# Scatter of experts 24 to 27, the overflow branch and the row loads moved ahead of the up products of experts 28 to 31

## The chip, the cores and the metric

The kernel runs on one core of a Trainium2 chip. A core has a tensor engine (PE; its weight loads are shown as PEld), a vector engine (VectorE, DVE), a scalar engine (ScalarE, ACT), GpSimd (POOL), a sync engine that issues most transfers (SP), and 16 DMA engines. The metric is device microseconds of one execution; lower is better.

## The reference, cut to what matters

Two layers follow each other. Each ends in a mixture of experts: every one of 384 tokens goes to the best two experts of one of four groups (32 experts in all, 1024 wide, 128 hidden), and the result is added to the residual and normalised.

```python
    hid = jax.nn.silu(jnp.einsum('td,edf->tef', t, w1)) * jnp.einsum('td,edf->tef', t, w3)
    hid = hid * gate[..., None].astype(hid.dtype)
    return jnp.einsum('tef,efd->td', hid, w2).reshape(B, L, D)
...
    y = hier_moe(x * (1 + sc2) + sh2, *moe_params)
    x = layer_norm(ALPHA * x + g2 * y, ln2_g, ln2_b)
```

## The kernel before, in words

`experts(l)` handles the experts in eight groups of four, q = 0 to 7. Each expert has room for 32 tokens; up to two experts of a group have a second 32. For each group:

- `ups(q, ...)` makes the up products in four steps (`up`, lines 1409 and 1415). VectorE and ScalarE first copy the weights of the two fuller experts into a buffer `hv` (line 1400).
- `hidden` is SiLU on ScalarE and a product on VectorE (line 1425); `hidden_T` transposes it on PE (lines 1430 and 1432) and VectorE copies it back as `hidT` (line 1436).
- `down(q)` makes three down products: z = 0 and z = 1 (line 1446) and the second slots, called z = 2 here (line 1453). ScalarE takes z = 0 from PSUM, VectorE z = 1, and ScalarE the second slots into the one buffer `ys2` (`y2` in the code). GpSimd scatters the rows by indirect DMA to `y_d` in memory (line 1458). As `ys2` has one buffer, the `y2` of a group is not written before the scatter of the `y2` before it has landed.

The tensor engine's order in the expert stage is the order of the code; for the other engines a scheduler sets it at build time from its own estimate of times. So a copy or a `y2` can stand far from its place in the code.

In the loop `ups(q)` stands ahead of `down(q - 1)`. The last group (q = 7) is different: its rows are not scattered. `down_keep(7)` keeps them in SBUF (`ysk`), and PE adds them by one-hot products (lines 1581 and 1583) to the three 128-token blocks. All other rows come back from memory: `load_yy` loads `y_d` into three tiles `yy` (line 1676), two rows a token. `ln2` adds the pairs (line 1691; one half on GpSimd, one on VectorE), adds PE's sums (line 1732) and normalises.

Between the last scatter and `load_yy` stands `overflow`: a branch (lines 1606 and 1607), taken only when an expert has more tokens than its slots hold. With these inputs it is not taken. Every engine loads the value and branches by itself. In the arm that is not taken each engine waits until its own earlier work is done, and then raises its semaphores by as much as the skipped body would have done.

Weights come in halves of 1 MB, the up weights into pools `raw` (6 buffers) and `wx` (4), the down weights `w2` into `wr` and one more buffer.

Of the kernel before, what the change touches and what calls it, by code (L numbers as in the profile page):

```python
# [8 lines left out]
F32 = mybir.dt.float32  # L9
# [11 lines left out]
D = 1024  # L21
NP, NS, T = 128, 256, 384
NT = 3
# [3 lines left out]
NQUAD = 8  # L27
# [52 lines left out]
class Kern:  # L80
# [1266 lines left out]
    def experts(self, l):  # L1347
        nc, mo, ep, tc = self.nc, self.mo, self.ep, self.tc
# [18 lines left out]
        def windows(q, ns=range(6)):  # L1367

            w = win[q]
            for n in ns:  # L1370
                at = first[4 * q + n] if n < 4 else more[q, n - 4]
                o, i_ = w[:, :, n * 32:(n + 1) * 32], xT[:, :, bass.ds(at, 32)]
                if n < 4:
                    self.act(o, i_, AF.Copy)
                else:
                    nc.vector.tensor_copy(o, i_)
            return w
# [50 lines left out]
        def hidden_T(hid):  # L1428
            pt = self.bank("ms")
            nc.tensor.transpose(pt[:, 0:128], hid[:, 0:2, :].rearrange("p h f -> p (h f)"), self.ident)  # L1430
            for h in range(2):
                nc.tensor.matmul(pt[h * 64:(h + 1) * 64, 128:192].rearrange("p (i r) -> p i r", i=2), hid[:, 2, :], ident4[:, :, h, :],
                                 start=True, stop=True)
            self.hidn += 1
            hT = hidTs[:, self.hidn % 2 * 192:self.hidn % 2 * 192 + 192]
            nc.vector.tensor_copy(hT, pt[:, 0:192])
            return hT
# [72 lines left out]
        def ups(q, kqs):  # L1510
            for kq in kqs:
                up(ps[q], q, kq, win[q])

        ps = {}
        with tc.manual_schedule(engines={e.engine for e in (nc.vector, nc.scalar, nc.tensor)}):
# [17 lines left out]
            hid = hidden(ps[0])  # L1533
            ups(1, (1,))
            hT = hidden_T(hid)
# [10 lines left out]
        with tc.manual_schedule(engines={nc.tensor.engine}):  # L1546
            self.slots()
            hid = hidden(ps[1])
            for z in range(4):
                evac(2, z, "AVAV"[z])  # L1550
            wn = self.hp.tile([128, 2, 8, 192], F32, tag="H", name="win")
            win += [wn[:, q % 2] for q in range(2, NQUAD)]
            windows(2)
            down(0, hT)
            for q in range(2, NQUAD):
                ps[q] = self.bank("mm")
                ups(q, (0, 1))
                hT = hidden_T(hid)
                ups(q, (2, 3))
                hid = hidden(ps[q])  # L1560
                if q < NQUAD - 1:
                    windows(q + 1)
                down(q - 1, hT)
            q, hT = NQUAD - 1, hidden_T(hid)
        self.ahead = self.NRAW
        self.overflow(l)
        self.load_yy(l)

        oT = [ep.tile([128, T], F32R, tag="hv", name="oT", bufs=2), self.eq.tile([128, 2, T], F32R, tag="ys", name="oT", bufs=2)]
        oT = [oT[0], oT[1][:, 0, :], oT[1][:, 1, :]]  # L1570
# [4 lines left out]
        ps = [[self.bank(("tp", "mm", "sc")[i]) for z in range(2)] for i in range(NT)]  # L1575
        with tc.manual_schedule(engines={nc.tensor.engine}):
            for i in range(NT):
                for z in range(2):
                    c = slice(i * 128, (i + 1) * 128)
# [24 lines left out]
    def overflow(self, l):  # L1604
        nc, a, mo, ep, tc = self.nc, self.a, self.mo, self.ep, self.tc
        most = nc.values_load(self.most[0:1, 0:1], min_val=0, max_val=T + CAP + 6 * CAP * T)
        with tc.If(most > 2 * CAP):
            wo = self.wrp.tile([128, 2048], F32, tag="wr", name="wo")
            part = lambda c, n: wo[:, c:c + NT * n].rearrange("p (i e) -> p i e", i=NT)
# [20 lines left out]
            for i in range(NT):  # L1630
                t = tt[:, 1, i, :]
                for d in range(8):
                    ps = self.bank("tp")
                    nc.tensor.transpose(ps[:, 0:128], t[:, d * 128:(d + 1) * 128], self.ident)
                    nc.vector.tensor_copy(tT[i][:, d * 128:(d + 1) * 128], ps[:, 0:128])
            with tc.For_i(0, NQUAD, 1) as it:
                nc.vector.tensor_copy(ixc, ix[:, :, bass.ds(it * 4, 4)])
                nc.vector.tensor_copy(gwc, gw[:, :, bass.ds(it * 4, 4)])
                w = [self.wx.tile([128, 2048], F32, tag="wx", name="w_ov") for _ in range(4)]
                for h in range(4):  # L1640
                    nc.sync.dma_start(w[h], a["w13"][bass.ds(it * 2 + (l * NHALF + h // 2), 1), h % 2].rearrange("o p c -> p (o c)"))
                w2 = [self.rawp.tile([128, 2048], F32, tag="raw", name="w2_ov") for _ in range(2)]
                for z in range(2):
                    nc.sync.dma_start(w2[z], a["w2"][bass.ds(it * 2 + (l * NHALF + z), 1)].rearrange("o p c -> p (o c)"))
                for e in range(4):
                    for i in range(NT):
                        ps = self.bank("mm")
                        for k in range(8):
                            c = e * 512 + k % 2 * 256
                            nc.tensor.matmul(ps[:, 0:256], tT[i][:, k * 128:(k + 1) * 128], w[k // 2][:, c:c + 256],  # L1650
                                             start=k == 0, stop=k == 7)
                        pv = ps[:, 0:256].rearrange("p (h m f) -> p h m f", h=2, m=2)
                        hid = ep.tile([128, 2, 64], F32, tag="hid", name="hidov", bufs=1)
                        self.act(hid, pv[:, :, 0, :], AF.Silu)
                        nc.vector.tensor_tensor(hid, hid, pv[:, :, 1, :], op=ALU.mult)
                        pt = self.bank("ms")
                        nc.tensor.transpose(pt[:, 0:128], hid.rearrange("p h f -> p (h f)"), self.ident)
                        hT = wo[:, 256:384]
                        nc.vector.tensor_copy(hT, pt[:, 0:128])
                        yo = wo[:, 1024:1024 + D]  # L1660
                        yv = yo.rearrange("p (h z c) -> p h z c", h=2, z=2)
                        for z in range(2):
                            po = self.bank("sc")
                            nc.tensor.matmul(po, hT, w2[z][:, e * 512:(e + 1) * 512], start=True, stop=True)
                            nc.vector.tensor_scalar(yv[:, :, z, :], po.rearrange("p (h c) -> p h c", h=2), gwc[:, i, e:e + 1], None, op0=ALU.mult)
                        nc.gpsimd.indirect_dma_start(
                            out=self.y_d, out_offset=bass.IndirectOffsetOnAxis(ap=ixc[:, i, e:e + 1], axis=0),
                            in_=yo, in_offset=None, bounds_check=2 * T - 1, oob_is_err=False)


    def load_yy(self, l):
        nc = self.nc
        self.yy = []
        for i in range(NT):
            t = self.rawp.tile([128, 2, D], F32, tag="raw", name="yy")
            nc.sync.dma_start(t, self.y_d.rearrange("(c t) d -> t c d", c=2)[i * 128:(i + 1) * 128])
            self.yy.append(t)

    def ln2(self, l, ps):
        nc, a, sm = self.nc, self.a, self.sm  # L1680
# [292 lines left out]
```

## Time and profile before

| what | us |
|---|---|
| median of 3 runs (lowest, highest) | 1128.95 (1126.01, 1133.52) |
| the profiled execution's own time | 1127.33 |
| its span, first to last instruction | 1125.6 |
| PE busy, share of the span | 1011.2, 90% |
| DVE busy, share of the span | 810.7, 72% |

The profiled execution is 1.62 us under the median; 1.73 us of its time lie outside the span. Busy times add over the engines, which work side by side; an idle engine costs time only where the end waits for it.

### The profile page before, as it was taken

To read this page: it belongs to the slowest core of one execution; us is meant where nothing else is said; L and a number is where in the kernel's file an instruction comes from. 1 tells how busy PE (TensorE), PEld (TensorE's weight loads), DVE (VectorE), ACT (ScalarE), POOL (GpSimd) and SP (SyncE) were. 2 spreads that over 40 slices of the span, in tenths; PEclk is the share of its full clock that TensorE was granted. 3 is DMA by queue.
4 is the path that set the end of the run, shared out by engine and by line. 5 is a ranking of instruction groups with operands and counts; after the bars stand their busy time and mean duration, and the time that the engine had idled before them with its cause. 6 is when DMAs were issued, how large, how long until landed. Compare 5 with 4: busy or idle time off the path is not lost. (4 is left out here: it accounts for less than half of the span.)

```text
span 1125.6 us, 20806 instructions
## 1 busy us (share of the span) xinstructions
PE 1011.2 (90%) x8182; PEld 840.7 (75%) x8182; DVE 810.7 (72%) x1530; ACT 417.4 (37%) x753; POOL 269.7 (24%) x232
## 2 busy tenths in 40 slices
PE   7999999999999999776689998999999999778673
PEld 5898978877999988433259897788999998754322
DVE  4399999965446986762569999997834587777437
ACT  4324254434333324341163443445532341434221
POOL 0001431221100510333244043114111025013335
PEclk9999999999999989897989999999999999989888
DMA  9967668447436667799585756773223666689955
GB/s 358 412 241 257 266 217 294 178 163 270 151 112 246 259 262 293 303 420 403 219 315 201 280 217 233 251 290 127 110 94 132 224 244 229 227 317 416 419 204 194
DMA packets 55101, 282.75 MB, mean 251 GB/s; under 512 B 8060, under 2 KB 12284, under 8 KB 27857
## 3 DMA queue, kind: packets, MB, share of 16 engines
q1 hardware_dynamic: 49632, 270.01, 63.1%
q0 software_dynamic: 5360, 11.29, 2.7%
q8 instruction: 69, 1.13, 0.4%
q14 instruction: 40, 0.32, 0.1%
HBM read 262.13 MB, written 24.71 MB: 255 GB/s over the span
## 5 line engine op out<-in xcount | busy, mean ns | idle before, releaser
L97 PE MATMUL ps_mm<-hThi,wr 128*128 128x384 f32 x672 | 229.9, 343 | 4.4 <-ACT hThi L102 2.3
L110 DVE TENSOR_TENSOR wr<-w_raw,wr 128x1024 fp32r<-128x1024 f32 x124 | 162.2, 1309 | 92.4 <-ACT wr L102 92.3
L98 PE MATMUL ps_mm<-hTlo,wr 128*128 128x384 f32 x672 | 228.0, 340 | 0.6 <-DVE hTlo L441 0.4
L99 PE MATMUL ps_mm<-hThi,wr 128*128 128x384 f32 x672 | 227.5, 339 | 0.6 <-DVE wr L110 0.6
L102 ACT ACTIVATE wr<-w_raw 128x1024 fp32r<-128x1024 f32 x140 | 147.5, 1055 | 68.1 <-PE ps_mm L99 37.8
L505 DVE SCALAR_TENSOR_TENSOR cacc<-pad,par,cacc 128x399 f32<-128x399 f32 x240 | 169.2, 705 | 4.2
L97 PEld LDWEIGHTS ps_mm<-hThi,wr 128*128 128x128 f32 x672 | 127.1, 189 | 18.2 <-issue 4.0
L98 PEld LDWEIGHTS ps_mm<-hTlo,wr 128*128 128x128 f32 x672 | 127.1, 189 | 6.3 <-DVE hTlo L441 2.5
L99 PEld LDWEIGHTS ps_mm<-hThi,wr 128*128 128x128 f32 x672 | 127.2, 189 | 2.5 <-DVE wr L110 0.9
L110 POOL TENSOR_TENSOR wr<-w_raw,wr 128x1024 fp32r<-128x1024 f32 x10 | 24.5, 2447 | 201.6 <-ACT wr L102 201.2
L1458 POOL DMA_INDIRECT y_d<-ys,dst x28 | 28.4, 1016 | 172.3 <-DVE hv L1400 73.3
L1446 PE MATMUL ps_sc<-w,hidT 128*32 128x512 f32 x256 | 43.1, 766 | 28.6 <-ACT ys L102 21.9
L1415 PE MATMUL ps_mm<-hv,win 128*32 128x128 f32 x1024 | 46.4, 277 | 9.2 <-DVE hv L1400 7.8
L1400 DVE COPY hv<-w_raw 128x512 f32 x60 | 41.9, 737 | 16.6 <-PE ps_mm L1415 10.8
L1415 PEld LDWEIGHTS ps_mm<-hv,win 128*32 128x32 f32 x1024 | 35.8, 112 | 22.7 <-DVE hv L1400 12.0
L1409 PE MATMUL ps_mm<-w_raw,win 128*32 128x256 f32 x640 | 47.8, 391 | 3.5 <-ACT win L102 3.5
L219 PE MATMUL ps_ms<-w_raw,cT 128*32 128x512 f32 x320 | 48.7, 612 | 1.4 <-DMA w_raw<-in_wada 1.4
L102 ACT ACTIVATE gate<-ps_mm 128x384 f32<-128x384 f32 x40 | 19.6, 490 | 81.6 <-PE ps_mm L99 80.5
L1446 PEld LDWEIGHTS ps_sc<-w,hidT 128*32 128x32 f32 x256 | 8.2, 123 | 45.8 <-ACT ys L102 32.9
L911 POOL TENSOR_TENSOR rtmp<-sc,lb 128x1024 f32<-128x1024 f32 x4 | 9.8, 2478 | 121.8 <-DMA lb<-in_ln 121.8
L842 POOL TENSOR_TENSOR merged<-merged,gate 128x384 f32<-128x384 f32 x16 | 18.1, 1135 | 87.0 <-DVE gate L841 87.0
L102 ACT ACTIVATE win<-xT 128x256 f32 x64 | 21.5, 409 | 37.6 <-PE ps_mm L1409 30.2
(505 smaller groups left out, 2355.7 us busy)
## 6 DMA issues: line engine op xcount, KB each, us to landing
w_raw<-in_wst SPq DMA_DIRECT2D x68, 1024.0 KB, 6.4
w_raw<-in_wada SPq DMA_DIRECT2D x48, 1024.0 KB, 5.4
w_raw<-in_w SPq DMA_DIRECT2D x40, 1024.0 KB, 10.7
w<-in_w SPq DMA_DIRECT2D x32, 1024.0 KB, 12.3
w_x<-in_w SPq DMA_DIRECT2D x24, 1024.0 KB, 11.8
bias<-in_bias SPq DMA_DIRECT2D x8, 768.0 KB, 7.6
y_d<-zero SPq DMA_DIRECT2D x2, 3072.0 KB, 15.1
yy<-y_d SPq DMA_DIRECT2D x6, 1024.0 KB, 7.1
```

Of the source, the lines that this page charges most:

```text
L97: mm(out, whi, xhi, start=first, stop=False)
L98: mm(out, whi, xlo, start=False, stop=False)
L99: mm(out, wlo, xhi, start=False, stop=last)
L102: return self.nc.scalar.activation(out, in_, f, **k)
L110: (eng or self.nc.vector).tensor_tensor(lo, x, hi.bitcast(F32), op=ALU.subtract)
L219: nc.tensor.matmul(ps[32 * t:32 * t + 32, :], self.cT[:, 2 * kp + k, :], w[:, t * 512:t * 512 + 512], start=(kp == 0 and k == 0), stop=(kp ...
L505: nc.vector.scalar_tensor_tensor(acc, pad[:, j:j + W], w, acc, op0=ALU.mult, op1=ALU.add)
L1400: nc.vector.tensor_copy(hv[:, i, :], src)
L1409: nc.tensor.matmul(ps[e * 32:(e + 1) * 32, 0:256], x[:, k, e * 32:(e + 1) * 32], w[:, e, kk, :], start=k == 0, stop=k == 7, skip_group_che ...
L1415: nc.tensor.matmul(ps[t * 32:(t + 1) * 32, 256:384], x[:, k, 128 + i * 32:160 + i * 32], hv[:, i, kk, h * 128:(h + 1) * 128], start=False, ...
L1446: nc.tensor.matmul(po[e * 32:(e + 1) * 32, :], hT[:, e * 32:(e + 1) * 32], w2[:, e, :], start=True, stop=True)
L1458: ins = nc.gpsimd.indirect_dma_start(out=view, out_offset=bass.IndirectOffsetOnAxis(ap=dst, axis=0), in_=rows, in_offset=None, bounds_chec ...
```

## The change

The last group's up products no longer stand between group 5's and group 6's down products. After the change PE runs `down(5)`, `hidden_T`, `down(6)`, the branch, `ups(7)`, `hidden_T`, `down_keep(7)`. The loads of `yy` are written ahead of `ups(7)` too. The tiles of `yy` are allocated earlier, and the body of the branch, which isn't run here, uses them for its weights.

```diff
-            for q in range(2, NQUAD):
+            last = NQUAD - 1
+            for q in range(2, last):
                 ps[q] = self.bank("mm")
                 ups(q, (0, 1))
                 hT = hidden_T(hid)
                 ups(q, (2, 3))
                 hid = hidden(ps[q])
-                if q < NQUAD - 1:
-                    windows(q + 1)
+                windows(q + 1)
                 down(q - 1, hT)
-            q, hT = NQUAD - 1, hidden_T(hid)
-        self.ahead = self.NRAW
+            down(last - 1, hidden_T(hid))
+
+        self.yy = [self.rawp.tile([128, 2, D], F32, tag="raw", name="yy") for _ in range(NT)]
         self.overflow(l)
         self.load_yy(l)
+        with tc.manual_schedule(engines={nc.tensor.engine}):
+            ps[last] = self.bank("mm")
+            ups(last, range(4))
+            q, hT = last, hidden_T(hidden(ps[last]))
+        self.ahead = self.NRAW
...
     def overflow(self, l):
...
+        spare = self.rawp.tile([128, 2048], F32, tag="raw", name="w_ov")
+        w = [t.rearrange("p c d -> p (c d)") for t in self.yy] + [spare]
+        w2 = [self.wx.tile([128, 2048], F32, tag="wx", name="w2_ov") for _ in range(2)]
         with tc.If(most > 2 * CAP):
```

On PE, layer 0, from the end of `down(5)` to the branch. Before (`w_5354` and `w_5356` are group 6's down weights, `w_x` and `w_raw` group 7's up weights):

```order
L1415 MATMUL ps_mm<-hv,win 32x128 [waits Activation_49]
...
L1409 MATMUL ps_mm<-w_raw,win 32x256 [waits DMAHW3_49]
...
L1446 MATMUL ps_sc<-w_5354,hidT 32x512 [waits DMAHW4_49,DVE_49]
L1446 MATMUL ps_sc<-w_5354,hidT 32x512 x3
L1446 MATMUL ps_sc<-w_5356,hidT 32x512 [waits DMAHW5_49,Activation_49]
L1453 MATMUL ps_sc<-hv,hidT 32x256 [waits DVE_49]
L1430 MATMUL ps_ms<-con,hid 128x128
L1432 MATMUL ps_ms<-con,hid 64x64 x2
L1606 TENSOR_LOAD most [waits DVE_49]
L1607 COMPARE_AND_BRANCH
```

After, the same place and on to the first up product of group 7 (the branch is lines 1612 and 1616 there):

```order
L1430 MATMUL ps_ms<-con,hid 128x128
L1432 MATMUL ps_ms<-con,hid 64x64 x2
L1446 MATMUL ps_sc<-w_5354,hidT 32x512 [waits DMAHW4_49,DVE_49,Activation_49]
L1446 MATMUL ps_sc<-w_5356,hidT 32x512 [waits DMAHW5_49,Activation_49]
L1453 MATMUL ps_sc<-hv,hidT 32x256 [waits DVE_49]
L1612 TENSOR_LOAD most [waits DVE_49]
L1616 COMPARE_AND_BRANCH
...
L1616 UNCONDITIONAL_BRANCH [waits PE_49]
L1409 MATMUL ps_mm<-w_x,win 32x256 [waits DVE_49,DMAHW6_49,PE_49,Activation_49]
L1409 MATMUL ps_mm<-w_x,win 32x256 x7
L1415 MATMUL ps_mm<-hv,win 32x128 x8
```

All of group 7's up products went behind the branch, and the first of them now waits for ScalarE's semaphore. In the built program this wait asks for a count of 350; ScalarE's last instruction ahead of the branch brings the count to 339, and ScalarE's own not-taken arm then adds 12. The product's PSUM bank is one that the skipped body reads on ScalarE.

On ScalarE, layer 0, up to the branch. Before (`ys_5345`, `ys_5480` and `ys_5605` are the `y2` of groups 4, 5 and 6; the `ys` of size 128x2x256 is z = 0 of group 6; ISA sets a register):

```order
L102 ACTIVATE hv<-w_x 128x512 [waits DVE_49,DMAHW7_49,PE_49,Activation_49]
L102 ACTIVATE ys_5345<-ps_sc,gate 128x512 [waits DMASW0_49,Activation_49]
L102 ISA
L102 ACTIVATE hv<-w_raw 128x512 [waits DMAHW2_49,DVE_49,PE_49]
L102 ACTIVATE hid<-ps_mm 128x192 [waits PE_49]
...
L102 ACTIVATE hv<-w_5356 128x512 [waits DMAHW5_49,DVE_49,Activation_49]
L102 ACTIVATE ys<-ps_sc,gate 128x2x256 [waits DMASW7_49,PE_49]
L102 ACTIVATE ys_5480<-ps_sc,gate 128x512 [waits DMASW2_49,Activation_49]
L102 ACTIVATE ys_5605<-ps_sc,gate 128x512 [waits DMASW4_49,PE_49,Activation_49]
L1606 TENSOR_LOAD most [waits DVE_49]
```

After (`ys_5525` is the `y2` of group 6):

```order
L102 ACTIVATE hv<-w_5356 128x512 [waits DVE_49,DMAHW5_49,PE_49,Activation_49]
L102 ACTIVATE ys_5345<-ps_sc,gate 128x512 [waits DMASW0_49,Activation_49]
L102 ACTIVATE ys<-ps_sc,gate 128x2x256 [waits DMASW7_49,PE_49]
L102 ISA
L102 ACTIVATE hv<-w_x 128x512 [waits DVE_49,DMAHW7_49,PE_49,Activation_49]
L102 ACTIVATE ys_5480<-ps_sc,gate 128x512 [waits DMASW2_49,Activation_49]
L102 ACTIVATE ys_5525<-ps_sc,gate 128x512 [waits DMASW4_49,Activation_49]
L1612 TENSOR_LOAD most [waits DVE_49]
L1616 COMPARE_AND_BRANCH
...
L102 ACTIVATE hv<-w_raw 128x512 [waits DMAHW2_49,DVE_49,PE_49]
L102 ACTIVATE hid<-ps_mm 128x192 [waits DVE_49,PE_49]
```

The second copy and the SiLU of group 7 went behind the branch and so behind the three `y2`, each of which waits (DMASW) for the scatter before it to land. Outside this stage the scheduler also puts instructions of layer 1's mixer in a slightly other order on all engines; which work is done is the same.

## Rows read from the trace of the kernel before

**Rows 1.** Timeline of PE, layer 0: start, duration, engine, line, operation, idle before.

```profile
533.28 1.07 PE L1409 MATMUL ps_mm<-w_raw,win 128*32 128x256 f32 x16
...
535.90 1.04 PE L1446 MATMUL ps_sc<-w,hidT 128*32 128x512 f32 x8
...
539.70 1.07 PE L1453 MATMUL ps_sc<-hv,hidT 128*32 128x256 f32 x16 [0.88 <-DVE ys L1473]
...
544.15 3.60 PE L1446 MATMUL ps_sc<-w,hidT 128*32 128x512 f32 x16 [2.86 <-PEq L1607]
```

**Rows 2.** Timeline of ScalarE, the same stretch.

```profile
529.71 0.63 ACT L102 ACTIVATE hv<-w_x 128x512 f32 x1 [4.91 <-PE ps_sc L1453]
530.25 0.67 ACT L102 ACTIVATE ys<-ps_sc,gate 128x512 f32<-128x512 f32 x1
...
538.52 0.69 ACT L102 ACTIVATE ys<-ps_sc,gate 128x512 f32<-128x512 f32 x1 [0.82 <-DMA y_d<-ys,dst]
545.07 0.69 ACT L102 ACTIVATE ys<-ps_sc,gate 128x512 f32<-128x512 f32 x1 [5.86 <-DMA y_d<-ys,dst]
```

**Rows 3.** Timeline of GpSimd, the same stretch: scatters of groups 4 to 6, a pair sum.

```profile
531.19 0.98 POOL L1458 DMA_INDIRECT y_d<-ys,dst  x1 [1.84 <-ACT ys L102]
...
541.66 1.18 POOL L1458 DMA_INDIRECT y_d<-ys,dst  x1 [0.30 <-issue]
546.03 0.98 POOL L1458 DMA_INDIRECT y_d<-ys,dst  x1 [3.18 <-ACTq L1607]
...
557.54 2.19 POOL L1691 TENSOR_TENSOR yy<-yy 128x512 f32<-128x512 f32 x1 [0.91 <-DMA yy<-y_d]
```

**Rows 4.** SyncE's queue, layer 0: load of `w_5356`, loads of `yy`.

```profile
509.75 0.33 SPq L342 DMA_DIRECT2D w<-in_w  x1
...
549.81 1.42 SPq L1676 DMA_DIRECT2D yy<-y_d  x3
```

**Rows 5.** Transfers issued from 506 to 512 us: count, KB each, median us to landing.

```profile
w<-in_w SPq DMA_DIRECT2D x2, 1024.0 KB, 21.0
```

**Rows 6.** The branch's own instructions, both layers: count, ns min/median/max, first and last start.

```profile
L1607 PEldq COMPARE_BRANCH  x2: 3342/3381/3420, 540.4 to 1085.8; - x2
...
L1607 ACTq EVENT_SEMAPHORE  x2: 17/17/17, 545.9 to 1091.2; - x2
```

**Rows 7.** Timeline of VectorE, layer 0.

```profile
536.52 0.35 DVE L1425 TENSOR_TENSOR hid<-hid,ps_mm 128x192 f32<-128x192 f32 x1
...
542.25 0.34 DVE L1436 COPY hidT<-ps_ms 128x192 f32<-128x192 f32 x1
...
554.79 0.69 DVE L1691 TENSOR_TENSOR yy<-yy 128x512 f32<-128x512 f32 x1 [3.58 <-DMA yy<-y_d]
555.59 0.69 DVE L1732 TENSOR_TENSOR x<-ps_tp,yy 128x512 f32<-128x512 f32 x1
...
558.53 1.75 DVE L1691 TENSOR_TENSOR yy<-yy 128x512 f32<-128x512 f32 x1
560.20 2.28 DVE L1701 SCALAR_TENSOR_TENSOR x<-r,x 128x1024 f32<-128x1024 f32 x1
...
563.93 1.23 DVE L1701 SCALAR_TENSOR_TENSOR x<-r,x 128x1024 f32<-128x1024 f32 x1
```

**Rows 8.** Timeline of all engines, the same place in layer 1.

```profile
1090.45 0.69 ACT L102 ACTIVATE ys<-ps_sc,gate 128x512 f32<-128x512 f32 x1 [6.67 <-DMA y_d<-ys,dst]
...
1090.62 3.55 PE L1446 MATMUL ps_sc<-w,hidT 128*32 128x512 f32 x16 [3.83 <-DVEq L1607]
...
1099.78 0.69 DVE L1691 TENSOR_TENSOR yy<-yy 128x512 f32<-128x512 f32 x1 [1.42 <-DMA yy<-y_d]
...
1100.58 0.69 DVE L1732 TENSOR_TENSOR x<-ps_tp,yy 128x512 f32<-128x512 f32 x1
```

**Rows 9.** Stretches: busy time by engine, granted PE clock (1.00 full), DMA share, GB/s.

```profile
522.00:526.00 4.00, 3.08 (x16) 0.40 (x16) 0.00 (x0) 0.75 (x2) 3.56 (x3) 0.50 0.98 379
...
544.20:549.00 4.80, 4.52 (x27) 0.74 (x27) 1.40 (x3) 2.56 (x4) 0.98 (x1) 0.64 0.04 8
```

More of the change, by code (lines that the diff above doesn't have):

```diff
@@ L1638, in overflow @@
                 nc.vector.tensor_copy(gwc, gw[:, :, bass.ds(it * 4, 4)])
-                w = [self.wx.tile([128, 2048], F32, tag="wx", name="w_ov") for _ in range(4)]
                 for h in range(4):
                     nc.sync.dma_start(w[h], a["w13"][bass.ds(it * 2 + (l * NHALF + h // 2), 1), h % 2].rearrange("o p c -> p (o c)"))
-                w2 = [self.rawp.tile([128, 2048], F32, tag="raw", name="w2_ov") for _ in range(2)]
                 for z in range(2):
@@ L1672, in load_yy @@
         nc = self.nc
-        self.yy = []
         for i in range(NT):
-            t = self.rawp.tile([128, 2, D], F32, tag="raw", name="yy")
-            nc.sync.dma_start(t, self.y_d.rearrange("(c t) d -> t c d", c=2)[i * 128:(i + 1) * 128])
-            self.yy.append(t)
+            nc.sync.dma_start(self.yy[i], self.y_d.rearrange("(c t) d -> t c d", c=2)[i * 128:(i + 1) * 128])
     def ln2(self, l, ps):
```

## The prediction

> **What bounds the kernel now.** PE is busy 90% of the span, but the change touches only the end of each layer's expert stage, some 45 us in each of two layers, so I read that stretch engine by engine from timelines and not from the shares. Three things are to be seen there.
>
> First, the end of the layer waits for rows that come back from memory. VectorE's first pair sum stands 3.58 us for the load of `yy` in layer 0 [rows 7] and 1.42 us in layer 1 [rows 8]. That load is issued at 549.81 [rows 4], 3.8 us after the last scatter began at 546.03 [rows 3].
>
> Second, that last scatter is late because the three `y2` follow each other through one buffer. The `y2` of group 5 waits until 538.52 for a scatter issued at 531.19, that of group 6 until 545.07 for one issued at 541.66 [rows 2, 3]: a landing costs 7.3 us while weights stream and 3.4 us once they have come.
>
> Third, PE's own jump over the branch body takes 3.34 and 3.42 us [rows 6]. Now it lies partly beside the copy of `hidT`, and PE stands 2.86 us (layer 0) and 3.83 us (layer 1, until VectorE's arm of the branch) ahead of the last group's down products [rows 1, 8].
>
> So at most 3.6 + 1.4 us of waiting for `yy` can go. Behind it lies a second cost: VectorE's sums of the next token block are held up by GpSimd's pair sums. The same pair sum took 0.69 us at 554.79 and 1.75 at 558.53, beside GpSimd's that ran from 557.54 for 2.19; the next long instruction took 2.28 against 1.23 for the same one later [rows 3, 7]. Earlier `yy` would free VectorE of 1.06 + 1.05 = 2.1 us a layer.
>
> **The change part by part.** I follow layer 0 on the clock of the trace before; nothing ahead of 528 us changes.
>
> *Group 6's down products come forward.* They start at 535.90 now [rows 1]. But the second half of group 6's weights, issued at 509.75, lands 21.0 us later, at 530.75 [rows 4, 5]; the up products of group 7 had hidden that. ScalarE now first copies this half, and only behind it, 0.54 us after the copy's start as at 529.71 and 530.25 [rows 2], writes group 4's `y2`, whose PSUM bank PE needs. So z = 0 starts about 532.0. From z = 0 to the end of z = 2 takes 539.70 + 1.07 - 535.90 = 4.9 us at the full clock [rows 1]: until 536.9, or 539.8 if the clock is at half, as it was from 522 to 526 [rows 9].
>
> *The branch moves to ScalarE's disadvantage.* Group 7's first up product waits for ScalarE's not-taken arm, and ScalarE comes to it only behind all `y2`. Group 4's scatter goes out 0.94 us after its `y2` began [rows 2, 3], at 532.2, and lands after 7.3 at 539.5. Group 5's `y2` takes 0.7, its scatter goes out at 540.5 and lands 3.2 us later (3.4 in the row, less because group 6's other scatter is long out of the way), so group 6's `y2` starts at 543.7. The arm ended 545.9 - 545.07 = 0.83 us after that start [rows 2, 6]: 544.5. PE starts group 7's up products at 544.6. It has then stood 4.8 to 7.7 us. PE's own jump is no bound: z = 2 began at 539.70 and the next work could start at 544.15 [rows 1], 4.45 later; here that is 540.3 to 543.2.
>
> The row says 3.3 us for PE's jump. [...]
>
> *Group 7's up products stand alone.* Two of the four steps took 535.90 - 533.28 = 2.62 us [rows 1], so four take 5.24. [...] 6.75 us, until 551.3. ScalarE's remaining copy for the third step is ready by then, since its arm ends just as PE starts.
>
> *Hidden values and their transposes are exposed.* Group 6's down products covered them. SiLU and product end 536.52 + 0.35 - 535.90 = 0.97 us behind the last up product [rows 7, 1]; transposes and copy took until 542.25 + 0.34 = 542.59 from PE's end of z = 2 at 540.77, 1.8 us with some queueing on VectorE [rows 1, 7]. I take 2.4 for both, with 2.8 as the upper end. `down_keep` starts at 553.7 and not at 544.15: 9.6 us late.
>
> *The end of the layer.* In layer 1 the first sum with PE's block began 1100.58 - 1090.62 = 10.0 us behind `down_keep`'s start, of which 1.42 was the wait for `yy` [rows 8] and 1.5 the return of the clock, which is already paid. That leaves 7.0. Rows of `yy` no longer wait: group 6's scatter goes out at about 544.7 and the load 3.8 later at 548.5, to be added before 560.7. So the sum of layer 0 starts at 560.7 and not at 555.59, 5.1 us late, less the 2.1 of GpSimd's hindrance and 0.4 of the wait between two sums: +2.7 us.
>
> *Layer 1* goes the same way: group 6's `y2` starts 1.4 us earlier than 1090.45, as in layer 0 (543.7 for 545.07), the arm ends 0.83 later, PE starts at 1090.0, `down_keep` at 1090.0 + 6.75 + 2.4 = 1099.1, the first sum at 1106.1 and not at 1100.58: 5.5 late, less 2.5, +3.0 us.
>
> *Loads and other queues.* SyncE's `yy` loads are issued 1.3 us earlier and the next layer's first weights with them, or once group 7 has released its buffers at 551.3 where they were issued at 551.35 before; I cost that at nothing. The scheduler's other order in layer 1's mixer has no row; PE is 9 tenths busy there, so I take 0 and 3 us either way.
>
> **Sum:** +2.7 + 3.0 = +5.7 us on 1127.33, 1133.0; the runs' median lies 1.6 above the profiled execution, so 1134.6, which I round to 1134.5.
>
> **Rivals.** *A, the stand is short, and the kernel gets faster.* If PE goes on as soon as its own jump is done, at 540.3, and not with ScalarE's arm, each layer saves 4.3 us: 5.7 - 8.6 = -2.9, 1126. For it: scatters could land sooner with fewer weights in flight. Against it: the count in the built program, and 7.3 us for the landing of one small scatter [rows 2, 3]. It decides if ScalarE passes its branch before 541.
>
> *B, PE stays at the lower clock, and the kernel is slower.* Work with gaps ran at 0.50 of full from 522 to 526 [rows 9] and the change adds gaps. If all four up steps run at half they take 10.5 and not 6.75 us, and if the pause for the hidden values drops the clock again `down_keep` pays its 1.5 too: 5.2 us a layer, 5.7 + 10.4 = +16, 1145. GpSimd's pair sums, now beside `down_keep`, could hold VectorE's copy of the last weights as well, by the 1.06 us of the held pair sum [rows 7]. It decides if the granted clock over the up products of group 7 is 0.5 throughout.
>
> *C, the mixer decides.* The other order in layer 1's mixer moves the time by more than 5 us, either way; one stall of PE on a late weight split would do it.
>
> **How the numbers follow.** The forecast, a small loss of 1 to 11 us, has 0.66; A 0.16, B 0.12, C 0.06. The range goes from A's 1126 to 1143, short of B. A measurement of this kernel can tell about 1%, 11 us, from no change: faster than 1117.7 only with C and A together, 0.03; slower than 1140.2 with B and the upper end of the forecast, 0.14; within 0.83.
>
> **What would show it.** In the changed kernel PE should stand 5 to 8 us ahead of the first `ps_mm` product of group 7, released by ScalarE's queue at the branch; `y2` of group 6 should start one to two us earlier than now; `down_keep` should start 8 to 10 us later; no pair sum should wait for `yy`, GpSimd's pair sums should be over before VectorE's first sum, and VectorE's second pair sum should take 0.7 us. I am wrong if PE is released by its own queue, if the lower clock covers all of group 7, or if the span of layer 1's mixer differs by more than 3 us.

## The result, and the profile after

| kernel | median of runs, us (lowest, highest) | profiled execution, its span |
|---|---|---|
| before | 1130.94 of 9 (1126.01, 1133.52) | 1127.33, 1125.6 |
| after | 1138.93 of 9 (1134.19, 1141.84) | 1138.93, 1137.1 |

The ratio after to before is 1.0076, 95% interval 1.0059 to 1.0093: 8 us or 0.8% slower, inside the 1% named as the bound of no change, and 4.4 us over the forecast of 1134.5. The interval leaves no doubt of a small loss. One execution of e4_chb (1656.75 us, granted clock 0.55) and one of e9_before_no_branch (1167.07 us, 0.82) ran slow as a whole and are left out of the medians and ratios below.

The line numbers of after: up products 1409 and 1415, down products 1446 and 1453, scatter 1458 and the copies on ScalarE 102 as before; the branch is 1616, the loads of `yy` 1681, VectorE's pair sums 1695, its first sum with PE's block 1736, its totals 1705. Group 5's first down product, the start of this place, stands at 521.29 and not at 522.11, so 0.82 us is to be added where a time of layer 0 is compared with the rows of before.

The timeline of PE, layer 0 (start, duration, engine, line, operation, idle before and its releaser); it answers to [rows 1]:

```profile
531.26 1.93 PE L1446 MATMUL ps_sc<-w,hidT 128*32 128x512 f32 x8 [1.68 <-ACT ys L102]
...
536.81 1.94 PE L1453 MATMUL ps_sc<-hv,hidT 128*32 128x256 f32 x16 [0.88 <-DVE ys L1473]
545.23 1.93 PE L1409 MATMUL ps_mm<-w_x,win 128*32 128x256 f32 x16 [6.49 <-ACTq L1616]
...
552.63 0.61 PE L1415 MATMUL ps_mm<-hv,win 128*32 128x128 f32 x16
554.40 0.33 PE L1430 MATMUL ps_ms<-con,hid 128*128 128x128 f32 x1 [1.16 <-DVE hid L1425]
...
555.46 1.92 PE L1446 MATMUL ps_sc<-w,hidT 128*32 128x512 f32 x16 [0.46 <-DVE hidT L1436]
```

PE ends z = 2 at 538.75 and stands 6.49 us, released by ScalarE's queue at the branch. `down_keep` (555.46) comes 11.3 us later than in [rows 1], 12.1 us counted from group 5. The page says the same for both layers in one of its costliest groups (busy and mean ns, then idle before and releaser):

```profile
L1409 PE MATMUL ps_mm<-w_x,win 128*32 128x256 f32 x384 | 28.7, 419 | 12.6 <-ACTq L1616 12.6
```

ScalarE and GpSimd in the same stretch, answering to [rows 2, 3], and SyncE's load, answering to [rows 4]:

```profile
538.90 0.63 ACT L102 ACTIVATE hv<-w_x 128x512 f32 x1 [4.95 <-PE ps_sc L1453]
539.44 0.67 ACT L102 ACTIVATE ys<-ps_sc,gate 128x512 f32<-128x512 f32 x1
544.35 0.69 ACT L102 ACTIVATE ys<-ps_sc,gate 128x512 f32<-128x512 f32 x1 [4.25 <-DMA y_d<-ys,dst]
```

```profile
540.38 0.98 POOL L1458 DMA_INDIRECT y_d<-ys,dst  x1 [1.87 <-ACT ys L102]
545.32 0.98 POOL L1458 DMA_INDIRECT y_d<-ys,dst  x1 [3.96 <-ACTq L1616]
```

```profile
549.24 2.08 SPq L1681 DMA_DIRECT2D yy<-y_d  x3
```

The branch's own instructions, answering to [rows 6] (count, ns least, median, most, first and last start): PE's jump and ScalarE's arm.

```profile
L1616 PEldq COMPARE_BRANCH  x2: 3768/3786/3805, 537.5 to 1088.9; - x2
L1616 ACTq EVENT_SEMAPHORE  x2: 17/17/17, 545.2 to 1096.4; - x2
```

PE's jump is over at 541.3; PE starts when ScalarE's arm is done. The last `y2` waits for the scatter of the one before, and behind it ScalarE's arm, PE's up products and the last scatter follow within a microsecond. Counted from group 5, the load of `yy` goes out 0.2 us later than before in layer 0 (549.24 + 0.82 for 549.81) and 0.7 us earlier in layer 1, although eight microseconds of up products now stand behind the branch.

The stretches (length, busy time by engine, granted PE clock, DMA share, GB/s), answering to [rows 9]: z = 0 to z = 2, the first two up steps, the last two:

```profile
531.20:538.80 7.60, 5.80 (x32) 1.00 (x32) 1.52 (x3) 0.69 (x2) 1.98 (x2) 0.50 0.71 280
545.20:549.50 4.30, 4.27 (x49) 2.37 (x52) 0.43 (x1) 0.63 (x1) 0.98 (x1) 0.50 0.03 8
549.50:553.30 3.80, 3.74 (x84) 2.60 (x76) 1.31 (x4) 0.00 (x0) 0.00 (x0) 0.86 0.79 259
```

Group 6's down products and the first half of group 7's up products run at a granted clock of 0.50 of full.

VectorE at the end of layer 0, answering to [rows 7]:

```profile
561.57 0.68 DVE L1695 TENSOR_TENSOR yy<-yy 128x512 f32<-128x512 f32 x1
562.36 0.69 DVE L1736 TENSOR_TENSOR x<-ps_tp,yy 128x512 f32<-128x512 f32 x1
...
565.12 0.69 DVE L1695 TENSOR_TENSOR yy<-yy 128x512 f32<-128x512 f32 x1
568.11 0.17 DVE L546 TENSOR_SCALAR chb<-par 128x8 f32<-128x8 f32 x1 [2.30 <-DMA par<-in_par]
568.19 1.22 DVE L1705 SCALAR_TENSOR_TENSOR x<-r,x 128x1024 f32<-128x1024 f32 x1
```

No pair sum of VectorE waits for `yy`, and GpSimd no longer holds VectorE (0.69 and 1.22 us for 1.75 and 2.28). But a row is there that the prediction did not have: `chb`, a small product of the next layer, stands ahead of the first total and waits 2.30 us for the load of `par`. The scheduler has put it there; before, it came behind the totals, at 569.5.

Layer 1, answering to [rows 8]:

```profile
1096.49 1.93 PE L1409 MATMUL ps_mm<-w_x,win 128*32 128x256 f32 x16 [6.13 <-ACTq L1616]
...
1105.87 2.63 PE L1446 MATMUL ps_sc<-w,hidT 128*32 128x512 f32 x16 [0.46 <-DVE hidT L1436]
...
1113.50 0.69 DVE L1736 TENSOR_TENSOR x<-ps_tp,yy 128x512 f32<-128x512 f32 x1
...
1118.92 0.69 DVE L1702 TENSOR_TENSOR x<-ps_mm,g 128x512 f32<-128x512 f32 x1 [0.64 <-PE ps_mm L1699]
```

To see where the time went I cut each profiled execution at group 5's first down product in both layers and at PE's first transpose of the next layer (line 405). Each column is worked out from the starts of these rows and the span; each kernel has one trace, and the middle alone differs by 2.6 us between two traces of after.

| kernel | end of layer 0 | middle: layer 1 up to group 5's down products | end of layer 1 |
|---|---|---|---|
| before | 45.8 | 499.1 | 58.6 |
| after | 53.5 | 498.1 | 64.2 |
| after, second trace (e7_after) | 53.2 | 495.6 | 64.1 |
| e1_arm, e8_arm_again | 53.1, 54.1 | 496.5, 497.0 | 60.5, 60.1 |
| e4_chb | 51.6 | 494.7 | 63.8 |
| e5_arm_chb | 49.9 | 494.3 | 60.5 |
| e5_order | 52.6 | 502.1 | 60.1 |
| e9_before_no_branch | 44.5 | 494.4 | 59.0 |
| e10_order_no_branch | 44.7 | 496.5 | 60.8 |
| e3_before_ys2 | 42.8 | 494.4 | 56.9 |
| e2_ys2 | 53.5 | 491.0 | 64.9 |
| e6_ys2_chb | 47.6 | 494.6 | 62.3 |
| e11_order_ys2 | 50.2 | 496.6 | 61.3 |

The two ends together are 13.3 us longer after the change (12.9 by the second trace), and the middle 1.0 to 3.5 us shorter. The middle can be cut once more, at layer 1's first up product. Ahead of it, in the mixer, where the scheduler's order differs, before takes 408.4 us and the two traces of after 405.7 and 404.5. Behind it, in groups 0 to 5 of the expert stage, the three take 90.7, 92.4 and 91.1 us.

### The profile page after: what moved, and what is told of

It reads as the page before. It is cut to its first block, busy times and chain, and to the rows that moved or that the text cites. A ratio compares the mean times of both kernels' runs of the same rounds, so it can differ in the third digit from the quotient of the medians.

```text
span 1137.1 us, 20827 instructions
## 1 busy us (share of the span) xinstructions
PE 1013.2 (89%) x8182; PEld 843.4 (74%) x8182; DVE 809.2 (71%) x1530; ACT 416.9 (37%) x753; POOL 267.8 (24%) x232
## 3 DMA queue, kind: packets, MB, share of 16 engines
q1 hardware_dynamic: 49632, 270.01, 62.3%
## 5 line engine op out<-in xcount | busy, mean ns | idle before, releaser
L110 DVE TENSOR_TENSOR wr<-w_raw,wr 128x1024 fp32r<-128x1024 f32 x124 | 165.2, 1334 | 92.5 <-ACT wr L102 92.3
L1400 DVE COPY hv<-w_raw 128x512 f32 x60 | 46.6, 820 | 31.5 <-PE ps_mm L1415 27.9
L1415 PE MATMUL ps_mm<-hv,win 128*32 128x128 f32 x1024 | 50.4, 285 | 12.1 <-DVE hv L1400 10.2
L1415 PEld LDWEIGHTS ps_mm<-hv,win 128*32 128x32 f32 x1024 | 38.6, 115 | 26.1 <-DVE hv L1400 14.9
L1409 PE MATMUL ps_mm<-w_raw,win 128*32 128x256 f32 x640 | 50.6, 404 | 2.9 <-ACT win L102 2.9
L219 PE MATMUL ps_ms<-w_raw,cT 128*32 128x512 f32 x320 | 44.7, 612 | 0.9 <-DMA w_raw<-in_wada 0.9
L1409 PE MATMUL ps_mm<-w_x,win 128*32 128x256 f32 x384 | 28.7, 419 | 12.6 <-ACTq L1616 12.6
```

Source lines behind the costliest of these rows:

```text
L110: (eng or self.nc.vector).tensor_tensor(lo, x, hi.bitcast(F32), op=ALU.subtract)
L219: nc.tensor.matmul(ps[32 * t:32 * t + 32, :], self.cT[:, 2 * kp + k, :], w[:, t * 512:t * 512 + 512], start=(kp == 0 and k == 0), stop=(kp ...
L1400: nc.vector.tensor_copy(hv[:, i, :], src)
L1409: nc.tensor.matmul(ps[e * 32:(e + 1) * 32, 0:256], x[:, k, e * 32:(e + 1) * 32], w[:, e, kk, :], start=k == 0, stop=k == 7, skip_group_che ...
L1415: nc.tensor.matmul(ps[t * 32:(t + 1) * 32, 256:384], x[:, k, 128 + i * 32:160 + i * 32], hv[:, i, kk, h * 128:(h + 1) * 128], start=False, ...
```

## The experiments

They ran in three series of four, each series beside runs of the kernel before on the same chip (medians 1127.80, 1130.54 and 1128.95).

| series | kernel | median, us | ratio to before, 95% interval |
|---|---|---|---|
| 1 | e1_arm | 1136.53 | 1.0073, 1.0053 to 1.0093 |
| 1 | e2_ys2 | 1130.01 | 1.0015, 0.9994 to 1.0036 |
| 1 | e3_before_ys2 | 1113.94 | 0.9880, 0.9860 to 0.9901 |
| 1 | e5_order | 1134.96 | 1.0053, 1.0034 to 1.0073 |
| 2 | e4_chb | 1136.31 | 1.0062, 1.0036 to 1.0087 |
| 2 | e5_arm_chb | 1129.39 | 0.9986, 0.9966 to 1.0006 |
| 2 | e6_ys2_chb | 1127.30 | 0.9974, 0.9951 to 0.9997 |
| 2 | e7_after | 1138.59 | 1.0084, 1.0051 to 1.0117 |
| 3 | e8_arm_again | 1136.32 | 1.0066, 1.0042 to 1.0090 |
| 3 | e9_before_no_branch | 1122.11 | 0.9942, 0.9922 to 0.9962 |
| 3 | e10_order_no_branch | 1125.45 | 0.9970, 0.9952 to 0.9989 |
| 3 | e11_order_ys2 | 1130.24 | 1.0024, 1.0007 to 1.0041 |

The theory was the prediction's: PE's stand for ScalarE's arm makes the loss. The rivals were that the stand only covers other waits, that the order of the products costs by itself, and that layer 1's mixer decides.

### e1_arm and e8_arm_again: PE no longer waits for ScalarE's arm

```diff
+                        nc.vector.tensor_copy(wo[:, 1024:1280], ps[:, 0:256])
-                        pv = ps[:, 0:256].rearrange("p (h m f) -> p h m f", h=2, m=2)
+                        pv = wo[:, 1024:1280].rearrange("p (h m f) -> p h m f", h=2, m=2)
```

The edit is in the body that is skipped. It takes only ScalarE off the PSUM bank.

> The changed kernel, but in the body of the branch (not run here) VectorE copies the up products out of PSUM and ScalarE reads the copy, so that the skipped body no longer has ScalarE read the bank that group 7's up products write; the order of the engines ahead of and behind the branch stays. Theory (PE stands for ScalarE's arm of the branch): PE starts group 7 when its own jump is done, 2.6 us behind the end of z = 2, at 541.4 and not 545.2 in layer 0; the third step still waits for a copy that ScalarE makes behind its arm, about 546, so the up products end about 549 and not 553.2. Some 3 to 4.5 us a layer less: 1130 to 1133. Rival 1 (the stand only covers what would be waited for anyway: the copy for the third step, the lower clock, the rows from memory): down_keep moves by less than 1 us, 1137 to 1140. Rival 2 (the loss comes from another order in layer 1's mixer): no stand shortened matters, 1138 to 1140.

> The kernel that took away only PE's wait for ScalarE's arm, once more. In the first call it came out level with the changed kernel (ratio 1.0073), though its trace was 5.8 us shorter; with the product of chb moved as well the next call gave 0.9986. Theory: the stand of 3.98 us for par is all that lies between the two, so this one should come to 0.9986 plus 4 of 1130 us, 1.002 to 1.005. Rival: something else in the moved product's place (GpSimd) matters, or calls differ by more than their intervals: 1.006 to 1.009 again.

The trace of e1_arm, PE and VectorE in layer 0:

```profile
541.31 1.94 PE L1409 MATMUL ps_mm<-w_x,win 128*32 128x256 f32 x16 [2.60 <-PEq L1616]
...
551.35 1.92 PE L1446 MATMUL ps_sc<-w,hidT 128*32 128x512 f32 x16 [0.46 <-DVE hidT L1436]
```

```profile
567.61 0.17 DVE L546 TENSOR_SCALAR chb<-par 128x8 f32<-128x8 f32 x1 [3.98 <-DMA par<-in_par]
```

and VectorE in the trace of e8_arm_again:

```profile
572.13 0.17 DVE L546 TENSOR_SCALAR chb<-par 128x8 f32<-128x8 f32 x1 [6.29 <-DMA par<-in_par]
```

The mechanism is shown: PE is released by its own jump, 3.9 us earlier, and `down_keep` stands at 551.35, 4.1 us earlier. The gain is not: layer 0's end is about as long as in after. In e1_arm VectorE comes to the wait for `par` 2.2 us earlier than in after (the rest of the 4.1 is lost ahead of it, where beside GpSimd's pair sums VectorE's copy of the last weights takes 1.37 us for 0.41), but `par` lets it go on only 0.5 us earlier. In e8_arm_again the wait is 4.0 us longer than in after. Layer 1 has no `par` to wait for, and its end is 3.7 to 4.1 us shorter. So I expected 6 to 9 us, and one layer's worth was left in the trace. The times show less, about 1 us under after by the ratios, each of which is known to some 2.5 us. The second run came out as its rival said, 1.0066, but for another reason than the rivals named: its stand for `par` was 6.29 and not 3.98 us.

### e4_chb, e5_arm_chb and e7_after: the wait for par taken out

```diff
-        nc.vector.tensor_scalar(hb, par[:, Q_CG:Q_CG + 8], 0.5, None, op0=ALU.mult)
+        (nc.gpsimd if l else nc.vector).tensor_scalar(hb, par[:, Q_CG:Q_CG + 8], 0.5, None, op0=ALU.mult)
```

e4_chb is after with this edit, e5_arm_chb is e1_arm with it. On all engines but these two the order is unchanged.

> The changed kernel with one small operation of the next layer (the 128x8 product that makes chb from par, line 546) on GpSimd in layer 1 instead of VectorE; nothing else moves on any engine. In the changed kernel the scheduler had put it ahead of VectorE's first total in layer 0, where it stood 2.30 us for the load of par. Theory (this stand is one term of the loss that the prediction did not have): the first total goes on at 565.9 and not at 568.2, layer 1 starts 2.3 us earlier, 1.5 to 2.5 us less than the changed kernel in the same call. Rival (something behind it, PE's sums of the next block or GpSimd's rstd, is as late): no difference, under 0.7 us.

> The kernel that took away PE's wait for ScalarE's arm, and the product of chb on GpSimd as well. In its trace PE had started group 7 by its own jump and down_keep 4.1 us earlier, but layer 1 only 0.5 us earlier, since VectorE then stood 3.98 us for par. Theory (the stand for ScalarE's arm does cost its 4 us a layer, and the load of par had eaten layer 0's share): layer 1 starts 3 to 4.5 us earlier than in the changed kernel's trace, and the time is 6 to 9 us under the changed kernel in the same call. Rival (the rows from memory, whose last scatter still goes out at 545.3, are the next wait): 0 to 3 us under it.

> The changed kernel itself once more, on the same chip as the three others, since single executions of it differ by some us: every difference is to be taken inside one call. Both theories: 7 to 9 us over the kernel before, as in the first comparison; its trace should again show PE standing some 6 us for ScalarE's queue in both layers, and VectorE some 2 us for par in layer 0.

e7_after repeats the loss, 8.1 us between the medians, with PE standing 6.00 and 6.19 us for ScalarE's queue and VectorE 2.19 us for `par`. Beside it e4_chb is 2.3 us less and e5_arm_chb 9.2 us less, both as the theory had it (9.2 a little over its 9). The 2.3 us alone lie inside the intervals and are not shown by the times; in the traces layer 0's end is 1.6 us shorter. The clearest pair is e4_chb and e5_arm_chb, which differ only in ScalarE's read of the bank:

```profile
546.25 1.94 PE L1409 MATMUL ps_mm<-w_x,win 128*32 128x256 f32 x16 [6.22 <-ACTq L1616]
```

```profile
542.41 1.94 PE L1409 MATMUL ps_mm<-w_x,win 128*32 128x256 f32 x16 [2.42 <-PEq L1616]
```

PE stands 3.8 us less in layer 0 and 3.5 us less in layer 1, the two ends together are some 5 us shorter, and the medians differ by 6.9 us (8.6 by the ratios, known to some 4). Here the wait for `par` no longer hides what the stand costs.

With the two waits gone the changed order is level with the kernel before, 0.9986. But it is level by two things. The ends are still 6.0 us longer than before, so the two waits make a little over half of their 13.3 us; the mixer of layer 1 is 4.5 us shorter (403.9 for 408.4). It is 2.7 to 4.5 us shorter in all six traces of the changed order with one buffer and the branch ahead, with the moved product or without, each against the one trace of before. No run has the moved product in the order of before. In e5_arm_chb's trace the wait for `par` has not vanished, it has gone to GpSimd:

```profile
569.63 0.27 POOL L546 TENSOR_SCALAR chb<-par 128x8 f32<-128x8 f32 x1 [7.97 <-DMA par<-in_par]
```

GpSimd's next work is the first block's reciprocal root, which VectorE needs; VectorE, done with the product before at 568.79, took the next at 570.95. So layer 0's end won 3.3 us, where PE had stood 3.6 us longer and VectorE 2.2. The middle is 0.9 to 3.8 us shorter in both kernels with the moved product than in the two traces of after; whether that is this product or the scatter of single traces is open.

### e2_ys2, e6_ys2_chb and e3_before_ys2: two buffers for the second slots' rows

```diff
-                    y2 = self.eq.tile([128, 512], F32, tag="ys2", name="ys2", bufs=1)
+                    y2 = self.eq.tile([128, 512], F32, tag=("ys2","ys3")[q%2], name="ys2", bufs=1)
```

> The changed kernel with two buffers for the second slots' rows (groups of even and of odd number), so that the last one waits for the scatter two back and not for the one before it. Theory: ScalarE comes to its branch at about 540.8 and not 545.0 in layer 0, PE goes on when its own jump is done (541.4), the copy for the third step is ready in time, and the load of rows is issued some 3.5 us earlier: down_keep 3.8 to 4.5 us earlier in each layer, 1129.5 to 1132. Rival 1 (the stand covers other waits): down_keep moves by less than 1 us, 1137 to 1140. A third outcome: two scatters at a time land later than one by one, and only half of it is kept, 1134.

> The changed kernel with two buffers for the second slots' rows, and the product of chb on GpSimd as well. In the trace with two buffers alone VectorE stood 4.35 us for par in layer 0. Theory: 3 to 4.4 us less than that kernel's 1130, 1126 to 1127 beside a kernel before at 1128, so 9 to 12 us under the changed kernel in the same call. Rival: PE's sums of the next block, which stood 3.38 us for VectorE there, hold it: under 1.5 us less, 1128.5 to 1130.

> The kernel before with the same two buffers. It tells how much of the wait for rows from memory can be had without moving anything. By the prediction's reading the last scatter goes out at about 542 and not 546, rows are there 4 us earlier, VectorE no longer stands 3.58 and 1.42 us for them, and GpSimd's pair sums are out of the way of VectorE's: 5 us from the waits and up to 4.2 from the pair sums, 1122 to 1126. Rival (something else is ready just behind the rows, as PE's sums): 0 to 3 us, 1128 to 1131.

The times of the first two came out as the theory had them, 1130.01, and 1127.30, 11.3 us under e7_after; for e2_ys2 that was luck. PE's up products do start by its own jump, with a stand of 1.99 us in layer 0 (at 538.60) and 4.91 in layer 1, and not by ScalarE's arm. But counted from group 5 `down_keep` comes 3.2 us earlier than in after in layer 0 and 0.7 us later in layer 1, and the two ends together are no shorter (118.4 us for 117.7). What e2_ys2 wins lies almost all ahead of group 5's down products: groups 0 to 5 take 87.8 and 86.7 us in the two layers, and 91.0 and 92.4 in after.

For e3_before_ys2 I was wrong, on the good side: 13.9 us less than before and not 2 to 6. The waits of PE over the whole span, before (engine, tile and line, releaser: us, times, longest):

```profile
PE ps_sc L1446 <- ACT ys L102: 21.9, 10, 6.3
```

and in e3_before_ys2:

```profile
PE ps_sc L1446 <- DMA w<-in_w: 17.4, 9, 5.4
...
PE ps_sc L1446 <- DVEq L1607: 5.6, 1, 5.6
PE ps_sc L1446 <- PEq L1607: 5.5, 1, 5.5
```

The one buffer had made PE wait all through the expert stage, since PE's z = 0 needs the bank that the late `y2` empties. With two buffers these waits go to the late weights and are shorter, and VectorE's wait for `yy` of [rows 7, 8] is gone. Groups 0 to 5 are 3.4 and 2.4 us shorter in the two layers, the ends 4.7 us together. Another 2.3 us come out of layer 1's mixer, where the scheduler's order changed too; whether the buffer has a part in those is open. This kernel is faster than both. I had read the chain of `y2` only at the last group.

It also shows what covers what. With two buffers the change costs 15 us by the ratios (e2_ys2 over e3_before_ys2) and not 8: PE's first down product of group 6 waits 4.98 us for its late weights, which group 7's up products cover in e3_before_ys2, and VectorE stands 4.35 us for `par`. In e6_ys2_chb, where neither VectorE's wait for `par` nor PE's for ScalarE's arm is left, the change still costs 10.6 us by the ratios against e3_before_ys2. So with two buffers most of the loss has another cause than the stand.

```profile
529.60 1.94 PE L1446 MATMUL ps_sc<-w,hidT 128*32 128x512 f32 x8 [4.98 <-DMA w<-in_w]
```

### e5_order and e11_order_ys2: the products reordered, the branch left behind them

```diff
             down(last - 1, hidden_T(hid))
-        self.yy = [self.rawp.tile([128, 2, D], F32, tag="raw", name="yy") for _ in range(NT)]
-        self.overflow(l)
-        self.load_yy(l)
-        with tc.manual_schedule(engines={nc.tensor.engine}):
             ps[last] = self.bank("mm")
             ups(last, range(4))
             q, hT = last, hidden_T(hidden(ps[last]))
+        self.yy = [self.rawp.tile([128, 2, D], F32, tag="raw", name="yy") for _ in range(NT)]
+        self.overflow(l)
+        self.load_yy(l)
```

> Half of the change: group 6's down products and scatter stand ahead of group 7's up products, but the branch and the loads of rows stand behind them, as before. Theory (the loss is the stand at the branch, not the order of the products): PE goes from z = 2 straight into the up products, at 538.8 in layer 0; ScalarE's arm lies beside them; only PE's own jump of 3.4 us stands behind the transposes, so down_keep starts about 550, 5.5 us earlier than in the changed kernel, in both layers: 1127 to 1131, level with the kernel before. Rival 1 (the order itself costs, since nothing covers the late down weights, the hidden values and the return of the clock): 1135 to 1139.

> The order of the products as changed, the branch behind group 7's up products as before, two buffers for the second slots' rows. With two buffers the kernel before came to 0.988 and the changed kernel to 1.0015 of the kernel before, 15 us apart. If the order of the products makes most of this (the late weights and the hidden values uncovered), it comes to 0.994 to 1.002. If the branch ahead of the up products makes it (its stand and the load of par behind VectorE), it comes to 0.986 to 0.992.

The theory failed here. `down_keep` came where it was expected (553.06; the stretch began 2.1 us late, so 551.0 on the clock of after), but the time is 6 us over before and not level. PE, then VectorE, in e5_order:

```profile
540.66 1.93 PE L1409 MATMUL ps_mm<-w_x,win 128*32 128x256 f32 x16
...
553.06 3.64 PE L1446 MATMUL ps_sc<-w,hidT 128*32 128x512 f32 x16 [3.91 <-PEq L1614]
```

```profile
558.15 1.50 DVE L1400 COPY hv<-w 128x512 f32 x1
...
561.79 1.48 DVE L1693 TENSOR_TENSOR yy<-yy 128x512 f32<-128x512 f32 x1
```

PE goes straight on, as expected, and stands later for its own jump, 3.91 us, behind which the 16 products take 3.64 us, as the 3.60 in [rows 1]. In layer 0 GpSimd's pair sums lie beside VectorE's copy of the last weights, which takes 1.50 us where after's took 0.41. The first sum comes 10.3 us behind `down_keep`, against 6.9 in after. In layer 0 the branch ahead of the up products thus saves behind `down_keep` most of what it costs ahead of it (the end is 0.9 us shorter here than in after). In layer 1 the copy is not held (0.43 us), and the end is 4.1 us shorter than after's. With two buffers e11_order_ys2 comes to 1.0024, just above the range given to the order of the products and level with e2_ys2: most of the 15 us are not due to the place of the branch.

### e9_before_no_branch and e10_order_no_branch: no branch at all

```diff
-        self.overflow(l)
```

in the kernel before and in e5_order. Both leave out the branch and its general path, which these inputs do not take.

> The kernel before without the branch and its general path, which these inputs do not take (the kernel could not serve other inputs). It prices PE's jump where it stood. Theory: behind the jump stands the wait for rows from memory, 3.58 and 1.42 us, and the scatter's landing is the same, so at most 1 to 3 us are gained over the kernel before. Rival: PE's stand of 2.86 and 3.83 us with the return of its clock (1.5 us each) is on the path: 6 to 9 us gained.

> Group 6's down products and scatter ahead of group 7's up products, as in the change, and no branch at all (the general path is left out, as in the run beside it). It prices the order of the products alone, against the same order as before without the branch. Theory as it stood in the prediction (the loss comes from the stand at the branch): down_keep starts about 547.5 in layer 0, rows are there by 553.5, the sum about 554.5: level with the other kernel without a branch, within 2 us. Rival (the up products of group 7 had covered the late down weights, the hidden values and the transposes, and no branch is needed for the loss): 4 to 8 us over it.

The order of the products alone costs 0.28% here, some 3 us, between "level" and the rival's 4 to 8; the two intervals just meet. In the traces it is 0.2 us at the end of layer 0 and 1.8 at that of layer 1. e9_before_no_branch gained 6.5 us, which its expectation gave to the rival. The trace doesn't bear that rival out: the ends together are only 0.9 us shorter, VectorE still waits for rows, and 4.7 us came out of the middle, where the scheduler had changed the order of the mixer. So this run does not price PE's jump. In the changed order the branch does cost: e10_order_no_branch is 9.4 us under e5_order by the ratios, and its ends are 7.2 us shorter.

```profile
556.27 0.69 DVE L1690 TENSOR_TENSOR yy<-yy 128x512 f32<-128x512 f32 x1 [1.15 <-DMA yy<-y_d]
```

## Why the prediction came out, step by step

*The direction: right, shown. The cause: right for about half of what the ends lost.* PE stands for ScalarE's arm (6.49 and 6.13 us, forecast 4.8 to 7.7). That the stand costs time is shown by e4_chb and e5_arm_chb, which differ in nothing else, 6.9 us. Taking it away alone gains nothing in layer 0, where the wait for `par` lies behind it. With both away the time is level with before, but 6.0 of the ends' 13.3 us remain and a shorter mixer makes up for them. Of these 6.0 the order of the products makes about 2 us (e10_order_no_branch against e9_before_no_branch, ends). The rest fits PE's own jump, for which PE stands 2.4 and 2.2 us in e5_arm_chb; its part was not measured alone. What fell is that the loss is only in the branch's new place: left behind the up products (e5_order) it is still 6 us. With two buffers the loss is larger and PE does not stand for ScalarE's arm at all (e6_ys2_chb against e3_before_ys2, 10.6 us).

*Group 6's down products:* z = 0 started 9.97 us behind group 5's, forecast 9.9. They ended 17.5 us behind it: of the two values that the prediction gave, the one at half clock (17.7) and not the one at full clock (14.8).

*ScalarE's arm* ended 0.85 us behind the start of the last `y2`, as taken (0.83), but that `y2` was 1.5 us late: the scatter ahead of it went out 0.7 us late and took 4.0 us to land and not 3.2. It was late because ScalarE's copy ahead of group 5's `y2` waited for PE's z = 2 until 538.90; the prediction had let that chain run without PE.

*Group 7's up products* took 8.0 us in layer 0 and 7.2 in layer 1, and not 6.75. The 1.5 us for a return of the clock, in this term and in the 7.0 behind `down_keep`, was my estimate from one row: 3.60 us for 16 products where twice 1.04 is 2.1 [rows 1], at a mean granted clock of 0.64 [rows 9]. No run shows such a price by itself; in its place the four steps took 2.8 and 1.9 us over the 5.24 at full clock, and in layer 0 the first two ran at 0.50 throughout. This is rival B in part; its condition, half clock over all of group 7, did not hold (0.86 and 0.98 over the last two steps of the two layers), and its price of 5.2 us was 1.3 and 0.4, with another 0.7 in layer 1 where `down_keep`'s first products took 2.63 us for 1.92. e5_order shows that the stand is not what brings the low clock: without it the first up step ran at the same 1.93 us. The down products ahead were at half already.

*Hidden values and transposes* 2.2 us, forecast 2.4; from `down_keep` to the first sum 6.9 and 7.6, forecast 7.0. The first sum was 7.6 us (layer 0) and 7.0 us (layer 1) late, counted from group 5, forecast 5.1 and 5.5.

*The savings behind it, 2.5 us a layer, are the step that failed.* (5.1 less 2.5 is 2.6; the 2.7 in the sum is a slip of 0.1.) The rows on which they rested did what was said (second pair sum 0.69, total 1.22). In layer 0 nothing of it was kept, 12.4 us from the first sum to the next layer for 12.3 before: VectorE's 2.30 us for `par` took it. The listing of the changed kernel's instructions had line 546 ahead of line 1705, and I had compared only the branch's surroundings there. In layer 1 1.4 us were kept; VectorE then stood 0.64 and 0.17 us for PE's sums, which `down_keep`'s lateness had delayed.

*The sum.* The ends cost 7.7 and 5.6 us in the trace and not 2.7 and 3.0: the terms were 7.6 us short. That the total of 8 us is nearer to the forecast of 5.6 is luck. Between the two profiled executions the middle gave 1.0 us back and the part ahead of group 5 0.8, and the profiled execution of before lay 3.6 us under the median of its nine runs. By the second trace of after the middle gave 3.5 us, more than the 3 that the forecast allowed the mixer. The mixer itself is 2.7 and 4.0 us shorter in the two traces of after; what in its order does it is not settled here.

*The rivals.* A was not what the change did; built as e1_arm it was worth 4.1 and 3.1 us at `down_keep` (4.3 was taken), but not at layer 0's end. C: the middle moved by less than 5 us. *Loads:* the load of `yy` was not 1.3 us earlier but 0.2 later in layer 0 and 0.7 earlier in layer 1. That the other loads cost nothing did not hold: `par` was there about as late as before, counted from group 5, but `chb` now waits for it ahead of the totals.

## What to carry to other kernels

The branch that isn't taken was still a meeting point here: PE's work behind it waited 6.49 and 6.13 us for ScalarE's arm, and so for what ScalarE had queued ahead of its arm. Before moving such a branch, ask which engine reaches it last and why; here it was a buffer of one, and doubling that buffer was worth 1.2% in the order of before. When a change moves instructions, read the new order up to the next layer's first wait: here a small product of the next layer ahead of the last sums, with its wait of 2.30 us, took away what had been won in layer 0.

## What the hardware showed that was not expected

In eight traces (before, after, e1_arm, e4_chb, e5_arm_chb, e5_order, e7_after, e11_order_ys2) PE's jump over the body took 3.3 to 3.8 us; in before and after the DMA share in its first 3.4 us was 0.29 to 0.33. In e2_ys2, e3_before_ys2 and e6_ys2_chb it took 3.4 to 6.2 us; in the first two the share over the stretches below was 0.41 to 0.53. In e3_before_ys2 and in e2_ys2 (count, ns least, median, most, first and last start):

```profile
L1607 PEldq COMPARE_BRANCH  x2: 5863/5978/6092, 534.8 to 1071.9; - x2
```

```profile
L1616 PEldq COMPARE_BRANCH  x2: 3379/4774/6169, 534.9 to 1079.2; - x2
```

against [rows 6], and the stretches of these jumps, first e3_before_ys2, then e2_ys2 (the last two numbers are DMA share and GB/s):

```profile
534.80:541.00 6.20, 0.90 (x13) 0.34 (x5) 2.58 (x9) 0.69 (x1) 2.06 (x2) 0.90 0.41 159
1071.90:1078.00 6.10, 1.10 (x17) 0.43 (x9) 2.74 (x10) 0.69 (x1) 2.05 (x2) 0.81 0.47 163
```

```profile
534.90:538.30 3.40, 1.70 (x16) 0.45 (x8) 3.04 (x8) 1.21 (x2) 1.54 (x2) 0.50 0.53 219
1079.20:1085.40 6.20, 1.55 (x20) 0.60 (x12) 2.77 (x8) 1.21 (x2) 1.94 (x2) 0.78 0.50 184
```

The three jumps of 5.9 to 6.2 us in these two traces lie beside 159 to 184 GB/s, but in e2_ys2 a jump beside 219 GB/s took 3.38 us, as long as those of before beside 103 and 112. What the long jumps waited for was not measured.

The load of `par`, 248 KB, landed 16.5, 10.7 and 12.0 us after its issue in before, e1_arm and e8_arm_again, and let VectorE go on 7.9 us after it in after: the earlier it was issued (552.96, 556.93, 560.07 and 560.17), the longer it mostly took. Counted from group 5 it was issued 30.9, 35.7, 35.4 and 38.9 us in and was there at 47.3, 46.4, 47.4 and 46.8: at nearly the same time, whenever it was issued. So PE's gain in e1_arm could not shorten layer 0 by more than this moved. The loads of 1 MB issued ahead of it took 11.9 to 13.4 us in the same stretch, which suggests that it waits behind them; no run takes them away.
